# Down-projection: when its weight sums are formed in HBM, and where its Strassen products are combined

## The chip, the cores and the metric

One core of one Trainium2 chip runs the whole program. The metric is device time in microseconds of that core for one launch, lower is better. TensorE (PE in the profile) multiplies; VectorE (DVE), ScalarE (ACT) and GpSimd (POOL) do the elementwise work; SyncE (SP), ACT and POOL issue DMAs. PSUM is the memory of eight banks into which TensorE accumulates, SBUF the working memory, HBM the outer one.

## The reference

One layer of a hybrid token mixer and a convolutional feed-forward block (FFN) on 512 latent tokens of width 1024, with 256 context tokens as a prefix. Cut to its frame:

```python
sh1x, sc1x, g1x, sh2x, sc2x, g2x = split((silu(c) @ w_ada + b_ada), 6)
hx  = modulate(rms_norm(x, norm1_g), sh1x, sc1x)
x   = x + g1x * token_mixer(hx, ..., s_f, s_b)   # (sigmoid(ga)*(a@w_br_a) + sigmoid(gb)*(ob@w_br_b)) @ w_o
hx2 = modulate(rms_norm(x, norm2_g), sh2x, sc2x)
a, val = split(hx2 @ w_up, (D_FF, D_FF))         # D_FF = 2816
a   = depthwise_conv_3x3(a) + conv_b             # on an 8 x 64 grid
x   = x + g2x * ((gelu(a) * val) @ w_down)       # w_down: 2816 x 1024
return rms_norm(x, final_norm_g)
```

All inputs and the output are float32. The change touches when some sums of blocks of `w_down` are formed, the product with `w_down`, and the last lines.

## The kernel before

**Products in three passes.** Each float32 weight block arrives in SBUF as `raw` (128 x 1024), is rounded by ACT to `wh` (L223) and DVE forms the remainder `wl = raw - wh` (L224). Activations are split in the same way into a high and a low part. A product is then three matmuls (high x high, high x low, low x high), so one weight costs 24 matmuls of 128x512.

**The weight stream.** `specs` lists 155 weight blocks in the order of use: heads (0 to 9), VS and U (10 to 25), GA with `w_br_a` (26 to 41), R (42 to 49), GB with `w_br_b` (50 to 65, the last gate stage), `w_o` (66 to 73), `ffn_w_up` (74 to 117) and `w_down` (118 to 154). `weights()` (L241) hands out the next one; each call also splits up to two blocks ahead and loads up to four ahead (`raw` has 4 slots, `wh` and `wl` 5 each). The loads are issued by SP, in order.

**The modulation.** The vectors `g1`, `sh2`, `sc2`, `g2` are not needed until late, so `ada2` (L1157) runs in the background of the middle stages: a POOL memset of four accumulators (L1164), their bias by SP (L1166), 64 loads of `w_ada` pieces by SP (L1172, `wa`), DVE additions (L1173), and for each accumulator a split (L349, L350) and two matmuls (L1180, L1181). In SP's queue `wa` loads and weight loads alternate, and in DVE's queue the additions and the `wl` splits.

**The Strassen stage.** `w_down` is split in five blocks of 512 rows (`BLOCKS`), each a 2 x 2 of quarters (256 rows by 512 columns), and a rest of two 128-row tiles (`TAIL`). The output is likewise 2 x 2: tokens 0 to 255 or 256 to 511 by columns 0 to 511 or 512 to 1023. In Winograd's form the blocks take seven products in place of eight; each product is a pair of PSUM banks (one per 128 tokens) into which 60 matmuls go. Four of the products multiply by sums of quarters, which are made in HBM: `sums_build()` has 40 steps of 512 KB, each a DMA that POOL issues, 20 that copy a quarter and 20 that add (L192, L194; ten of these read another sum). `weights()` takes one step per call from the third call on. On the other side `all_preps()` forms the sums of activations and splits them. After each product DVE combines it with the earlier ones in SBUF: `taken` is an ACT copy of a bank, `combine` (L1557) a DVE addition or subtraction of a bank and a tile; `out_add` (L1501, L1502) multiplies by the gate `g2` and adds to the residual `x1`. Banks are taken in turn from two pools, `mm` and `gl`, of four each.

**The tail.** For each tile of 128 tokens `out_tok` ends the row: the sum of squares on ACT (L1507), `n3b` on DVE (L1518), the root on ACT (L1519), its reciprocal on DVE (L1520), then the left half times it on ACT (L1522, L1523 the DMA), the right half on DVE (L1524, L1525 the DMA). The last matmuls belong to tiles 2, 3, 0, 1 in this order.

What sets the order on an engine is the order in which the program is written out, moved by a scheduler; `in_order` pins some of it.

## Time and profile before

| | |
|---|---|
| median of 3 runs | 930.86 us (930.39 to 930.86) |
| profiled execution: its own time | 931.05 us |
| its span | 929.3 us |
| TensorE busy, of the span | 98% |
| DVE, ACT, POOL busy | 74%, 43%, 5% |
| granted TensorE clock | 0.999 |
| HBM read, written | 137.88 MB, 23.07 MB |

Times in the profile count from the span's start; the execution's own time holds the span and what lies around it. A row of the chain of waits is one piece of the work that ended last, with its start and length. Matmuls are pipelined: the 0.39 us of one is its way through, and the distance from start to start is what it costs. Times of landing are from a DMA's issue. "SPq", "POOLq" and "ACTq" are the queues of engines that issue DMAs.

### The profile page before, as it was taken

To read this page: it belongs to the slowest core of one execution; us is meant where nothing else is said; L and a number is where in the kernel's file an instruction comes from. 1 tells how busy PE (TensorE), PEld (TensorE's weight loads), DVE (VectorE), ACT (ScalarE), POOL (GpSimd) and SP (SyncE) were. 2 spreads that over 40 slices of the span, in tenths; PEclk is the share of its full clock that TensorE was granted. 3 is DMA by queue.
4 is the path that set the end of the run, shared out by engine and by line. 5 is a ranking of instruction groups with operands and counts; after the bars stand their busy time and mean duration, and the time that the engine had idled before them with its cause. 6 is when DMAs were issued, how large, how long until landed. Compare 5 with 4: busy or idle time off the path is not lost.

```text
span 929.3 us, 12172 instructions
## 1 busy us (share of the span) xinstructions
PE 913.0 (98%) x4540; PEld 761.3 (82%) x4540; DVE 690.7 (74%) x1197; ACT 400.8 (43%) x669; POOL 42.3 (5%) x74
## 2 busy tenths in 40 slices
PE   7999999999999999999999999999999999999996
PEld 5778888888888887788888888888888888888885
DVE  5578687779798644379665445898787878999796
ACT  5357465556542223223223226643343334465734
POOL 1200100010011112100000000000000000000000
PEclk9999999999999999999999999999999999999999
DMA  9951710662359999995452350533333333356642
GB/s 281 333 150 26 246 48 1 205 202 92 91 182 238 262 233 222 249 289 182 136 173 87 101 187 10 155 110 91 107 98 91 91 102 103 102 171 202 187 131 90
DMA packets 158615, 140.76 MB, mean 151 GB/s; under 512 B 6825, under 2 KB 122869, under 8 KB 158557
## 3 DMA queue, kind: packets, MB, share of 16 engines
q1 hardware_dynamic: 149197, 117.72, 41.4%
q0 software_dynamic: 8672, 21.19, 10.0%
q10 hardware_dynamic: 688, 1.09, 0.3%
q8 instruction: 35, 0.57, 0.2%
q14 instruction: 23, 0.19, 0.1%
HBM read 137.88 MB, written 23.07 MB: 173 GB/s over the span
## 4 chain that ended last, share of the span: by engine, by line
PE 85%; DMA 6%; DVE 4%; SPq 3%; ACT 1%; issue 1%; DVEq 0%; ACTq 0%
PE mm L357 48%; PE mm L375 11%; PE gl L1535 6%; PE mm L1535 4%; DMA wa<-in_w_ada_dram 3%; PE gl L881 3%; DMA raw<-in_w_in_dram 2%; SPq L273 1%; PE mm L988 1%; PE mm L1038 1%; PE mm L651 1%; PE gl L375 1%; DVE wl L224 1%; DVE vsn L1134 1%; SPq L294 1%; PE gl L916 1%
## 5 line engine op out<-in xcount | busy, mean ns | idle before, releaser
L223 ACT CAST wh<-raw 128x1024 fp32r<-128x1024 f32 x154 | 161.7, 1054 | 316.0 <-PE mm L357 180.9
L224 DVE TENSOR_TENSOR wl<-raw,wh 128x1024 fp32r<-128x1024 f32 x154 | 186.8, 1219 | 73.7 <-ACT wh L223 73.1
L357 PE MATMUL mm<-h2l,wh 128*128 128x512 f32 (+1 forms) x344 | 133.1, 387 | 0.0
L357 PE MATMUL mm<-h2h,wh 128*128 128x512 f32 (+1 forms) x344 | 133.1, 387 | 0.0
L357 PE MATMUL mm<-h2h,wl 128*128 128x512 f32 (+1 forms) x344 | 133.1, 387 | 0.0
L1392 DVE SCALAR_TENSOR_TENSOR cacc<-ca,ccol,cacc 128x441 f32<-128x441 f32 (+2 forms) x176 | 121.8, 694 | 4.1
L357 PE MATMUL mm<-hxh,wh 128*128 128x512 f32 x296 | 116.2, 392 | 0.0
L357 PE MATMUL mm<-hxh,wl 128*128 128x512 f32 x296 | 115.5, 390 | 0.0
L357 PE MATMUL mm<-hxl,wh 128*128 128x512 f32 x296 | 115.5, 390 | 0.0
L357 PEld LDWEIGHTS mm<-h2h,wl 128*128 128x128 f32 x344 | 64.6, 188 | 13.2
L357 PEld LDWEIGHTS mm<-h2h,wh 128*128 128x128 f32 x344 | 64.6, 188 | 13.1
L357 PEld LDWEIGHTS mm<-h2l,wh 128*128 128x128 f32 x344 | 64.6, 188 | 13.0
L1173 DVE SCALAR_TENSOR_TENSOR acc<-wa,cs,acc 128x512 f32<-128x512 f32 x64 | 46.0, 744 | 34.7 <-DMA wa<-in_w_ada_dram 34.6
L357 PEld LDWEIGHTS mm<-hxh,wl 128*128 128x128 f32 x296 | 55.6, 188 | 11.6
L357 PEld LDWEIGHTS mm<-hxh,wh 128*128 128x128 f32 x296 | 55.6, 188 | 11.1
L357 PEld LDWEIGHTS mm<-hxl,wh 128*128 128x128 f32 x296 | 55.6, 188 | 11.1
L1393 ACT ACTIVATE cacc<-cacc 128x512 f32<-128x512 f32 x22 | 13.9, 632 | 50.3 <-DVE cacc L1392 50.3
L375 PE MATMUL mm<-wh,hxh 128*128 128x512 f32 x88 | 34.7, 395 | 0.0
L375 PE MATMUL mm<-wl,hxh 128*128 128x512 f32 x88 | 34.4, 391 | 0.0
L375 PE MATMUL mm<-wh,hxl 128*128 128x512 f32 x88 | 34.3, 390 | 0.0
L1535 PE MATMUL gl<-wl,dah 128*128 128x512 f32 x80 | 31.1, 389 | 0.0
L1535 PE MATMUL gl<-wh,dah 128*128 128x512 f32 x80 | 31.1, 389 | 0.0
(429 smaller groups left out, 1729.9 us busy)
## 6 DMA issues: line engine op xcount, KB each, us to landing
raw<-in_w_in_dram SPq DMA_DIRECT2D x52, 512.0 KB, 4.3
wa<-in_w_ada_dram SPq DMA_DIRECT2D x96, 256.0 KB, 5.3
raw<-in_ffn_w_up_dram SPq DMA_DIRECT2D x44, 512.0 KB, 3.7
sum<-in_ffn_w_down_dram POOLq DMA_DIRECT2D x30, 512.0 KB, 6.1
raw<-sum SPq DMA_DIRECT2D x20, 512.0 KB, 3.8
raw<-in_ffn_w_down_dram SPq DMA_DIRECT2D x17, 512.0 KB, 3.6
sum<-sum POOLq DMA_DIRECT2D x10, 512.0 KB, 8.4
raw<-in_w_br_a_dram SPq DMA_DIRECT2D x8, 512.0 KB, 7.1
```

The lines of the kernel that those rows point to most:

```text
L223: A.copy(wh, raw)
L224: V.tensor_tensor(wl, raw, wh.bitcast(F32), op=ALU.subtract)
L273: dma(t_, w_ada[0, kp * nk * P:(kp + 1) * nk * P, c0:c0 + cg].rearrange("(k p) c -> p k c", p=P))
L294: dma(fqk[k // 2][0][:, j, k % 2], wi[k * P:(k + 1) * P, c0:c0 + P])
L357: T.matmul(ps, a[:, k, :], b[:, c0:c0 + n], start=(k == 0 and i == 0), stop=(k == KT - 1 and i == 2))
L375: T.matmul(ps, a[:, t * P:(t + 1) * P], b[:, k % 2, :], start=(k == 0 and i == 0), stop=(k == KT - 1 and i == 2))
L651: T.matmul(fps[i], a, b, start=(k == 0 and z == 0), stop=(k == KT - 1 and z == 2))
L881: T.matmul(ps, p_, q_, start=(start and z == 0), stop=(stop and z == 2))
L1173: V.scalar_tensor_tensor(acc[j], w_, cs[:, k, 0:1], acc[j], op0=ALU.mult, op1=ALU.add)
L1392: V.scalar_tensor_tensor(o, a_[:, r0 + dy:r1 + dy, c0 + dx:c1 + dx], wcol(tap), o, op0=ALU.mult, op1=ALU.add)
L1393: A.activation(acc, acc, AF.Gelu)
L1535: T.matmul(ps, a, w[:, kk, c0:c0 + n_], start=(first and kk == 0 and i == 0), stop=(last and kk == 1 and i == 2))
```

## The change

1. The 40 steps of `sums_build()` begin at weight 60 (`SUMS0`) and not at weight 2, one per call, so they go with weights 60 to 73 and 76 to 101 (74 and 75 are taken without a call).
2. The Strassen products keep their PSUM banks: X and Z are the `gl` pairs, Y is an `mm` pair. The first product M1 goes into X and is copied; M5 into Z and is copied; M6 is accumulated onto M1 in X, copied (`u2`) and subtracted from the right half of tokens 0 to 255; the third goes into Y with the first rest; X and Z go on accumulating likewise, with one copy or one `combine` between. `specs` and `all_preps()` follow the new order, and the last two quarters in row 1, column 1 come after the second sums.
3. The first rest's weights are held until both token halves have used them.
4. `out_tok` returns its last four operations as `finish`; tile 0's are run within tile 1's.

```diff
@@ -32,6 +32,7 @@
 TAIL = FT - 4 * BLOCKS
 LEAD = 5
 EARLY = 8
+SUMS0 = 60
 
 
@@ -171,14 +172,22 @@
     def w_block(ap):
         specs.append((ap.rearrange("(k p) c -> p k c", p=P), 2, 512))
 
-    by_block = lambda f: [w_block(f(b)) for b in range(BLOCKS)]
-    by_block(lambda b: quarter(b, 0, 0))
-    for i in range(4):
-        by_block(lambda b: sums[b][i])
-    for col in range(2):
-        by_block(lambda b: quarter(b, 1, col))
+    by_block = lambda f, b0=0, b1=BLOCKS: [w_block(f(b)) for b in range(b0, b1)]
+
+    def w_rest(col):
         for k in range(2 * BLOCKS, FT // 2):
             w_cols(ffn_w_down[0], col * 512, 512, 2 * k, 2)
+
+    by_block(lambda b: quarter(b, 0, 0))
+    by_block(lambda b: sums[b][0])
+    by_block(lambda b: sums[b][1])
+    by_block(lambda b: quarter(b, 1, 0))
+    w_rest(0)
+    by_block(lambda b: sums[b][3])
+    by_block(lambda b: quarter(b, 1, 1), 0, BLOCKS - 2)
+    by_block(lambda b: sums[b][2])
+    by_block(lambda b: quarter(b, 1, 1), BLOCKS - 2)
+    w_rest(1)
 
     def sums_build():
         for step in (((0, (0, 1)), (1, (1, 1)), (2, (1, 0)), (3, (0, 1))), ((0, (0, 0)), (3, (1, 1))),
@@ -241,7 +250,7 @@
     def weights():
         i = pos[2]
         pos[2] += 1
-        if i > 1:
+        if i >= SUMS0:
             next(building, None)
         stream_split(i + 2)
         stream_load(i + 1 + AHEAD)
@@ -1451,15 +1460,21 @@
         for b in range(BLOCKS):
             yield act_both(kept[b])
         for b in range(BLOCKS):
-            yield act_both(quads(b)[3])
+            yield act_both(quads(b)[1])
         for b in range(BLOCKS):
             a11, _, a21, _ = quads(b)
             yield act_both(tile_op(a11, a21, ALU.subtract))
+
+        def last(b):
+            V.tensor_tensor(kept[b], quads(b)[1], kept[b], op=ALU.add)
+            return act_both(kept[b])
+
+        for b in range(BLOCKS - 2):
+            yield last(b)
         for b in range(BLOCKS):
-            yield act_both(quads(b)[1])
-        for b in range(BLOCKS):
-            V.tensor_tensor(kept[b], quads(b)[1], kept[b], op=ALU.add)
-            yield act_both(kept[b])
+            yield act_both(quads(b)[3])
+        for b in range(BLOCKS - 2, BLOCKS):
+            yield last(b)
 
     preps, ready = all_preps(), []
 
@@ -1493,13 +1508,13 @@
         wh, wl = w
         for i, (a, b) in enumerate(((gh, wh), (gh, wl), (gl_, wh))):
             T.matmul(ps, a[:, t * P:(t + 1) * P], b[:, kk, c0:c0 + n], start=(first and i == 0),
-                     stop=(last and i == 2))
-
-    def out_add(pv, hf, t, c0, n):
+                     stop=(last and i == 2), skip_group_check=True)
+
+    def out_add(pv, hf, t, c0, n, op=ALU.add):
         tmp = late([P, n], s="yt")
         xv = x1[t][hf][:, c0:c0 + n]
         V.tensor_tensor(tmp, pv, bc_g["g2", hf][:, c0:c0 + n], op=ALU.mult)
-        V.tensor_tensor(xv, xv, tmp, op=ALU.add)
+        V.tensor_tensor(xv, xv, tmp, op=op)
         return tmp, xv
 
     def out_step(pv, hf, t, c0, n, part):
@@ -1519,10 +1534,14 @@
         A.activation(r, ss3[:, t, before:before + 1], AF.Sqrt, bias=b_, scale=1.0 / D)
         V.reciprocal(r, r)
         in_order(start, V.engine)
-        A.mul(xg[t], xg[t], r)
-        adma(out[0, t * P:(t + 1) * P, 0:512], xg[t])
-        V.scalar_tensor_tensor(x1[t][1], x1[t][1], r, fng[1], op0=ALU.mult, op1=ALU.mult)
-        dma(out[0, t * P:(t + 1) * P, 512:1024], x1[t][1])
+
+        def finish():
+            A.mul(xg[t], xg[t], r)
+            adma(out[0, t * P:(t + 1) * P, 0:512], xg[t])
+            V.scalar_tensor_tensor(x1[t][1], x1[t][1], r, fng[1], op0=ALU.mult, op1=ALU.mult)
+            dma(out[0, t * P:(t + 1) * P, 512:1024], x1[t][1])
+
+        return finish
 
     n, todo = [0], []
 
@@ -1533,7 +1552,7 @@
             hi, lo = (y.rearrange("p k t -> p (k t)")[:, c:c + P] for y in (ah, al))
             for i, (a, w) in enumerate(((hi, wh), (hi, wl), (lo, wh))):
                 T.matmul(ps, a, w[:, kk, c0:c0 + n_], start=(first and kk == 0 and i == 0),
-                         stop=(last and kk == 1 and i == 2))
+                         stop=(last and kk == 1 and i == 2), skip_group_check=True)
 
     def operands():
         prep(n[0] + LEAD)
@@ -1542,15 +1561,13 @@
         n[0] += 1
         return z
 
-    def products(bank, blocks=BLOCKS, stop=True):
-        banks = [bank() for _ in range(2)]
+    def products(banks, first=True, stop=False, blocks=BLOCKS):
         for b in range(blocks):
             z = operands()
             for t in range(2):
-                product_in(banks[t], t, 0, 512, z, b == 0, stop and b == blocks - 1)
+                product_in(banks[t], t, 0, 512, z, first and b == 0, stop and b == blocks - 1)
             if todo:
                 todo.pop(0)()
-        return banks
 
     def combine(a, b, op):
         t_ = late([P, 512], s="dc")
@@ -1562,51 +1579,64 @@
         A.copy(t_, ps)
         return t_
 
-    m1 = [taken(z) for z in products(gl)]
-    m5 = products(gl)
-    m6 = products(mm)
-    u2 = [combine(m, z, ALU.add) for z, m in zip(m6, m1)]
-    w5 = [combine(z, u, ALU.subtract) for z, u in zip(m5, u2)]
-    m4 = products(mm)
-    u4 = [combine(u, z, ALU.add) for u, z in zip(u2, m4)]
-    m7 = products(gl)
-    c21 = [combine(u, z, ALU.add) for u, z in zip(u4, m7)]
-    e22 = [combine(w, z, ALU.subtract) for w, z in zip(w5, m7)]
-    for t in range(4):
-        todo.append(lambda t=t: out_add((w5 + e22)[t], 1, t, 0, 512))
-    def rest_in(ps, t, c0, n_, w, first):
+    def rest_in(ps, t, w, first):
         for k in range(TAIL):
-            down(ps, gs[k], w[k // 2], k % 2, t, c0, n_, first and k == 0, k == TAIL - 1)
-
-    acc = products(gl, stop=False)
+            down(ps, gs[k], w[k // 2], k % 2, t, 0, 512, first and k == 0, k == TAIL - 1)
+
+    def left(t, src):
+        out_step(src, 0, t, 0, 512, 0)
+        xg.append(late([P, 512], s="xg"))
+        V.tensor_tensor(xg[t], x1[t][0], fng[0], op=ALU.mult)
+
+    X, Z = [gl() for _ in range(2)], [gl() for _ in range(2)]
+    Y = [mm() for _ in range(2)]
+    products(X)
+    m1 = [taken(z) for z in X]
+    products(Z, stop=True)
+    m5 = [taken(z) for z in Z]
+    products(X, False)
+    u2 = [taken(z) for z in X]
+    for t in range(2):
+        todo.append(lambda t=t: out_add(u2[t], 1, t, 0, 512, ALU.subtract))
+    products(Y)
     w = [weights() for _ in range(TAIL // 2)]
     start = len(traced())
     for g_ in gact:
         gs.append(split_act(g_.rearrange("p r w -> p (r w)"), s="g", lo_pool=late, eng=A.copy))
     A.activation(small(1, "root"), eps_t, AF.Sqrt)
     in_order(start, A.engine)
-    for t in range(4):
-        ps = acc[t] if t < 2 else mm()
-        rest_in(ps, t, 0, 512, w, t > 1)
-        e = (m1 + c21)[t]
-        V.tensor_tensor(e, ps, e, op=ALU.add)
-        out_step(e, 0, t, 0, 512, 0)
-        xg.append(late([P, 512], s="xg"))
-        V.tensor_tensor(xg[t], x1[t][0], fng[0], op=ALU.mult)
-
+    for t in range(2):
+        rest_in(Y[t], t, w, False)
+        left(t, combine(Y[t], m1[t], ALU.add))
+    products(X, False)
+    e22 = [combine(m, z, ALU.subtract) for m, z in zip(m5, X)]
+    for t in range(2):
+        todo.append(lambda t=t: out_add(e22[t], 1, t + 2, 0, 512))
     first = BLOCKS - 2
-    acc = products(mm, first, False)
+    products(Z, False, blocks=first)
+    products(X, False)
+    for t in range(2):
+        rest_in(X[t], t + 2, w, False)
+        left(t + 2, X[t])
     zs = [operands() for _ in range(BLOCKS - first)]
     w = [weights() for _ in range(TAIL // 2)]
     for t in (2, 3):
-        ps = gl()
-        rest_in(ps, t, 0, 512, w, True)
-        out_tok(t, lambda: out_step(ps, 1, t, 0, 512, 1), 1)
+        ps = mm()
+        rest_in(ps, t, w, True)
+        out_tok(t, lambda: out_step(ps, 1, t, 0, 512, 1), 1)()
+    ends = []
     for t in range(2):
         for z in zs:
-            product_in(acc[t], t, 0, 512, z, False, False)
-        rest_in(acc[t], t, 0, 512, w, False)
-        out_tok(t, lambda: out_step(acc[t], 1, t, 0, 512, 1), 1)
+            product_in(Z[t], t, 0, 512, z, False, False)
+        rest_in(Z[t], t, w, False)
+
+        def part():
+            out_step(Z[t], 1, t, 0, 512, 1)
+            while ends:
+                ends.pop()()
+
+        ends.append(out_tok(t, part, 1))
+    ends.pop()()
 
 
 # ---- launch: one core; inputs and outputs as the reference has them ----
```

**Where instructions move.** Three places, before and after apart. POOL, at the modulation's accumulators (`acc`) and the sums in HBM (`sum`); before:

```order
L192 DMA sum_128<-in_ffn_w_down_dram 256x512
L192 DMA sum_131<-in_ffn_w_down_dram 256x512
L1164 MEMSET acc_2952 128x512
L1164 MEMSET acc_2955 128x512
L1164 MEMSET acc_2958 128x512
L1164 MEMSET acc_2961 128x512
L192 DMA sum_132<-in_ffn_w_down_dram 256x512
```

after the change:

```order
L1173 MEMSET acc_2935 128x512
L1173 MEMSET acc_2938 128x512
L1173 MEMSET acc_2941 128x512
L1173 MEMSET acc_2944 128x512
L1173 MEMSET acc_3979 128x512
L1173 MEMSET acc_3982 128x512
L1173 MEMSET acc_3985 128x512
L1173 MEMSET acc_3988 128x512
L201 DMA sum_115<-in_ffn_w_down_dram 256x512
L201 DMA sum_116<-in_ffn_w_down_dram 256x512
```

The first memsets stood behind 17 sums and the second four behind 39; now all eight stand ahead of the first sum.

TensorE, at the change from the second Strassen product to the third (matmul 3888; `dah`, `dal` are the split sums of activations); before:

```order
L1535 MATMUL gl_7440<-wl_7515,dah_7443 128x512
L1535 MATMUL gl_7440<-wh_7514,dal_7444 128x512
L1535 MATMUL mm_7554<-wh_7536,dah_7466 128x512
L1535 MATMUL mm_7554<-wl_7537,dah_7466 128x512
L1535 MATMUL mm_7554<-wh_7536,dal_7467 128x512
```

after the change:

```order
L1554 MATMUL gl_7339<-wl_7517,dah_7445 128x512
L1554 MATMUL gl_7339<-wh_7516,dal_7446 128x512
L1554 MATMUL gl_7336<-wh_7538,dah_7468 128x512
L1554 MATMUL gl_7336<-wl_7539,dah_7468 128x512
L1554 MATMUL gl_7336<-wh_7538,dal_7469 128x512
```

The matmuls are the same; the third product went into a new bank (`mm_7554`) and now goes into the first product's (`gl_7336`), which an ACT copy has read.

DVE, the last rows of the program (x_1049 is the right half of token tile 0, x_1051 that of tile 1); before:

```order
L1501 TENSOR_TENSOR yt_8247<-mm_8118,g_1025_4928 128x512
L1502 TENSOR_TENSOR x_1049_5075<-x_1049_5075,yt_8247 128x512
L1518 TENSOR_SCALAR n3b_8245<-ss_7335 128x1
L1520 RECIPROCAL n3r_8246<-n3r_8246 128x1
L1524 TENSOR_SCALAR x_1049_5075<-x_1049_5075,n3r_8246,fng_7333 128x512
L1501 TENSOR_TENSOR yt_8278<-mm_8119,g_1025_4928 128x512
L1502 TENSOR_TENSOR x_1051_5079<-x_1051_5079,yt_8278 128x512
L1518 TENSOR_SCALAR n3b_8276<-ss_7335 128x1
L1520 RECIPROCAL n3r_8277<-n3r_8277 128x1
L1524 TENSOR_SCALAR x_1051_5079<-x_1051_5079,n3r_8277,fng_7333 128x512
```

after the change:

```order
L1516 TENSOR_TENSOR yt_8229<-gl_7338,g_1025_4890 128x512
L1541 TENSOR_SCALAR x_1055_5053<-x_1055_5053,n3r_8197,fng_7333 128x512
L1517 TENSOR_TENSOR x_1049_5041<-x_1049_5041,yt_8229 128x512
L1533 TENSOR_SCALAR n3b_8227<-ss_7335 128x1
L1535 RECIPROCAL n3r_8228<-n3r_8228 128x1
L1516 TENSOR_TENSOR yt_8256<-gl_7339,g_1025_4890 128x512
L1517 TENSOR_TENSOR x_1051_5045<-x_1051_5045,yt_8256 128x512
L1541 TENSOR_SCALAR x_1049_5041<-x_1049_5041,n3r_8228,fng_7333 128x512
L1533 TENSOR_SCALAR n3b_8254<-ss_7335 128x1
L1535 RECIPROCAL n3r_8255<-n3r_8255 128x1
L1541 TENSOR_SCALAR x_1051_5045<-x_1051_5045,n3r_8255,fng_7333 128x512
```

Tile 0's last product (L1524, now L1541) moved behind tile 1's addition, and tile 3's (x_1055) into tile 0's part.

## The prediction

> **What bounds the kernel now.** I read the page first, then the chain of waits from its end backwards, then TensorE's waits, and only then the rows around them.
>
> ```profile
> PE 913.0 (98%) x4540; PEld 761.3 (82%) x4540; DVE 690.7 (74%) x1197; ACT 400.8 (43%) x669; POOL 42.3 (5%) x74
> ```
>
> TensorE is busy for 98% of the span of 929.3 us, so anything that saves work on DVE, ACT or a queue is worth only what it takes out of TensorE's gaps. The chain of waits (start, length, what; longest pieces) says where these are:
>
> ```profile
> 334.34 8.75 DMA wa<-in_w_ada_dram
> ...
> 348.11 8.79 DMA wa<-in_w_ada_dram
> 357.00 0.76 DVE acc L1173
> ...
> 362.81 16.31 DMA raw<-in_w_in_dram
> ...
> 385.01 97.99 PE mm L357 x432
> ...
> 587.44 228.51 PE mm L357 x1008
> ...
> 922.06 0.70 DVE yt L1501
> ...
> 924.80 0.75 DVE x L1524
> ```
>
> From 385.01 us to the last matmul the chain is TensorE alone: 432 matmuls in 97.99 us, 0.2268 us each, 5.44 us for the 24 matmuls of one weight. Nothing that the change does to DVE there can bring a gain. Before 385 the chain goes through loads: the modulation loads `wa` (8.75 and 8.79 us) and one weight load of 16.31 us, with DVE sums of the modulation between. TensorE's own waits (total, times, longest) show what of that it felt:
>
> ```profile
> PE gl L1181 <- DVE accl L350: 1.4, 2, 1.1
> PE gl L1180 <- ACT acch L349: 0.6, 2, 0.3
> PE gl L1096 <- DVE swl L350: 0.3, 1, 0.3
> ```
>
> The first two are the modulation product of `ada2`; their idle times are counted from modelled ends of pipelined matmuls, so I measure the loss from start to start in TensorE's timeline (start, length, line):
>
> ```profile
> 357.81 0.39 PE L357 MATMUL mm<-ah,wl 128*128 128x512 f32 x1
> ...
> 359.18 0.50 PE L1181 MATMUL gl<-accl,ones_r 128*128 128x512 f32 x1 [0.23 <-DVE accl L350]
> 359.52 0.39 PE L357 MATMUL mm<-hxh,wh 128*128 128x512 f32 x1
> ```
>
> ```profile
> 382.14 0.39 PE L357 MATMUL mm<-ah,wl 128*128 128x512 f32 x1
> ...
> 384.51 0.51 PE L1181 MATMUL gl<-accl,ones_r 128*128 128x512 f32 x1 [1.14 <-DVE accl L350]
> 384.85 0.40 PE L357 MATMUL mm<-hxh,wh 128*128 128x512 f32 x1
> ```
>
> Each piece holds three matmul steps, worth 3 x 0.2268 = 0.68 us. The first takes 359.52 - 357.81 = 1.71 us (1.03 lost), the second 384.85 - 382.14 = 2.71 (2.03 lost): 3.06 us in all.
>
> **The change part by part. The sums leave 98 to 400 us.** Who makes the loads late is seen in the DMA queues of the stretch 318:357 (packets, MB, share of 16 engines; then issues, KB, median us to landing):
>
> ```profile
> q0 software_dynamic: 1683, 3.22, 51.1%
> ...
> wa<-in_w_ada_dram SPq DMA_DIRECT2D x12, 256.0 KB, 8.8
> ```
>
> and in 404:440, where POOL's queue is nearly empty:
>
> ```profile
> wa<-in_w_ada_dram SPq DMA_DIRECT2D x11, 256.0 KB, 5.1
> ```
>
> The software queue, which carries the sums, takes half of all DMA time there. The loads form a ring: a batch of four `wa` is issued, lands, DVE adds it, splits the next weight, and this frees the slots for the next batch. Its period was 348.11 - 334.34 = 13.77 and 362.81 - 348.11 = 14.70 us, while TensorE eats two weights in 2 x 5.44 = 10.89. With landings of 5.1 in place of 8.75 and 8.79 the periods are about 10.1 and 11.0, so the ring keeps up. The two rounds alone bring the modulation's `acc` some 7.3 us forward, and the first loss was 1.03; at the second the load of 16.31 us shrinks as well. Bounds of this term: 0 (the ring has another limit) and -3.52 (the wait of L1096 at 261 us goes too, 0.46 from start to start; but its chain is DVE's own work, so I leave it). I take **-3.06**, the value at the end nearest the rows, since less than a sixth of the expected lead would suffice at the first place.
>
> The Trainium skill ("DMA: Bandwidth & Descriptors", section "Queues, rings and completion order") says that each DMA engine takes turns between the queues that have work, a packet batch at a time. By it a load beside a sum takes up to twice its time alone, so `wa` would land in 4.4 us and the periods be 9.5 and 10.3; the measured ratio is 8.8 to 5.1, 1.7, and the sum would be the same.
>
> **The sums arrive at about 490 to 730 us.** Forty steps, one per weight of 5.44 us: six in the last gate stage, eight in `w_o`, 26 in the FFN. What one costs is the software queue's time over the span divided by 40: 10.0% of 929.3 / 40 = 2.3 us of all 16 engines, thus 2.3 / 5.44 = 0.43 of the DMA's time more.
>
> ```profile
> q0 software_dynamic: 8672, 21.19, 10.0%
> ...
> raw<-in_ffn_w_up_dram SPq DMA_DIRECT2D x44, 512.0 KB, 3.7
> ```
>
> ```profile
> 600.00:640.00 40.00, 40.00 (x178) 33.14 (x177) 36.07 (x54) 17.29 (x24) 0.00 (x0) 1.00 0.32 94
> ```
>
> The row of the windows (us; busy PE, PEld, DVE, ACT, POOL; clock; DMA share; GB/s) gives 0.32 there, so 0.75 with the sums. What hides it is the lead of the weight loads (SP's and ACT's timelines):
>
> ```profile
> 644.75 33.01 SPq L211 DMA_DIRECT2D raw<-in_ffn_w_up_dram  x7
> ```
>
> ```profile
> 663.44 1.06 ACT L223 CAST wh<-raw 128x1024 fp32r<-128x1024 f32 x1 [3.23 <-PE mm L357]
> ```
>
> The first of these seven loads is the one that the cast at 663.44 reads (`raw` has four slots, and the three casts between belong to the loads before): 18.7 us after its issue, 15.0 after its landing, and what releases the cast is TensorE, not the load. If a sum brings the landing to 8.8, 10 us of cover are left. The cast itself runs four weights (21.8 us) ahead of its use. A landing of over 18 us would be needed before even a cast is late: cost **0**. The finished sums are first read at about weight 120 (after 815 us); the last is issued near weight 99.
>
> **The modulation's memsets** now stand ahead of all sums in POOL's queue; nothing waits behind a sum there any more. A gain at most, and the same 3.06.
>
> **The Strassen stage** has the same 468 matmuls of 128x512, and ten DVE additions fewer against four ACT copies more. TensorE is dense there, so the ten (about 0.68 us each) are worth 0. Can the new order stop it? A bank goes on accumulating only after its copy: X is read after its first product and written again 60 matmuls (13.6 us) later, the shortest gap is the 36 matmuls (8.2 us) into Z between two uses of X, and a copy or an addition takes 0.6 to 0.7 us:
>
> ```profile
> L1562 ACT COPY dt<-gl 128x512 f32<-128x512 f32 x2 | 1.2, 584 | 0.1
> L224 DVE TENSOR_TENSOR wl<-raw,wh 128x1024 fp32r<-128x1024 f32 x32 | 38.9, 1219 | 7.2 <-ACT wh L223 6.7
> L1557 DVE TENSOR_TENSOR dc<-dc,gl 128x512 f32<-128x512 f32 x4 | 2.5, 678 | 0.0
> ```
>
> The weight pair of the first rest is held from matmul 4008 to 4187, so four of five pairs turn over. From a freed pair to its next need are then 36 matmuls, 8.2 us, against 0.42 (matmul start to reader, 922.06 - 921.64) + 1.06 (cast) + 1.22 (`wl`) = 2.7: 5.5 us to spare. The tightest place is where DVE waits for the last matmul into X (4079) to form `e22`, with six operations and a `wl` behind it that TensorE needs at 4117: 38 x 0.2268 = 8.6 us against 0.42 + 6 x 0.68 + 1.22 = 5.7, so 2.9 to spare. Cost **0**, bounds 0 and what the third rival gives.
>
> **The tail.** Token tile 0's last multiplications and output DMAs are moved behind tile 1's addition. DVE's 0.75 (L1524) then lies between tile 1's `x` and its `n3b`, while ACT squares:
>
> ```profile
> 921.64 0.39 PE L1495 MATMUL mm<-wh,gl 128*128 128x512 f32 x1
> ...
> 923.40 0.15 DVE L1518 TENSOR_SCALAR n3b<-ss 128x1 f32<-128x1 f32 x1
> 923.51 0.63 ACT L1507 ACTIVATE yt<-x 128x512 f32<-128x512 f32 x1 [2.07 <-DVE x L1502]
> 924.27 0.29 ACT L1519 ACTIVATE n3r<-ss,n3b 128x1 f32<-128x1 f32 x1
> ...
> 924.80 0.72 ACT L1522 ACTIVATE xg<-xg,n3r 128x512 f32<-128x512 f32 x1 [0.23 <-DVE n3r L1520]
> ...
> 925.55 0.37 ACTq L1523 DMA_DIRECT2D out_dram<-xg  x1
> ```
>
> `n3b` ends near 924.2 instead of 923.55, and is needed at 924.27: just hidden. But ahead of it tiles 2 and 3 now share their additions, which by my reckoning with these durations pushes tile 0's reciprocal to about 922.05, the moment at which tile 1's `yt` may start; that costs about 0.2. Tile 0's output DMAs are then issued some 1.4 us before the last ones, instead of four, and may share DMA time with them: 0 to 0.3. Bounds 0 and 1.84 (0.75 of DVE, 0.72 of ACT's multiplication and 0.37 of its issue all in series); I take **+0.3**.
>
> **Sum**: 931.05 (the profiled execution's own time) - 3.06 + 0 + 0 + 0.3 = 928.3. The median of the runs, 930.86, lies 0.19 below that execution, so **928.1 us** on it, 0.30% less. About 0.2%, 1.86 us, is what a measurement of this kernel can tell from no change: under 929.0 is faster, over 932.7 slower.
>
> **The rivals.** 1. *The ring stays bound by something else.* For it: the page's row of DMA shares (40 slices of 23.2 us, in tenths) is full from the thirteenth slice to the eighteenth, 279 to 418 us, and SP's own loads, let go earlier, could fill what the sums leave:
>
> ```profile
> DMA  9951710662359999995452350533333333356642
> ```
>
> Against: the software queue's 51.1%, and 5.1 us landings with as many loads but no sums. If only the second loss goes, 931.05 - 2.03 + 0.3 - 0.19 = 929.1; if neither, 931.2. It decides if two rounds gain under 1 us together.
>
> 2. *The tail takes the bound of 1.84*: 930.86 - 3.06 + 1.84 = 929.6. For it: reciprocal and `yt` meet within 0.1 us in my reckoning. Against: most of the moved work has ACT and DVE idle to run in.
>
> 3. *Slower: DVE is behind in the Strassen stage.* Its place is the `wl` behind `e22` (and the same after the first rest). For it: DVE is nearly full at its entry,
>
> ```profile
> 820.00:860.00 40.00, 40.00 (x179) 33.10 (x178) 38.24 (x50) 25.33 (x34) 0.00 (x0) 1.00 0.67 201
> ```
>
> with 1.76 us idle of 40. Each microsecond of backlog over 2.9 stops TensorE for one. Slower by the bound needs a stall of 3.06 - 0.3 + 1.86 = 4.6, a backlog of 7.5. At 10 us the stall is 7.1 and the time 928.1 + 7.1 = 935.2. Against: the change takes 10 x 0.68 = 6.8 us off DVE in this very stage.
>
> 4. *Slower: each sum that POOL issues in the FFN holds DVE.* DVE has 3.9 us idle of 40, thus 13.8 in the 141 us of 26 weights, and 21.8 - 2.3 = 19.5 us of lead; so it takes 33.3 / 26 = 1.28 us for each sum before TensorE waits. At two issue lengths (1.76 each, 45.8 in all) the end is 12.5 us late: 940.6. Against, in the timelines of POOL and DVE:
>
> ```profile
> 333.05 0.88 POOL L194 DMA_DIRECT2D sum<-in_ffn_w_down_dram  x1 [1.05 <-DVE acc L1173]
> ```
>
> ```profile
> 332.66 2.35 DVE L224 TENSOR_TENSOR wl<-raw,wh 128x1024 fp32r<-128x1024 f32 x2
> ```
>
> two `wl` with the issue of a sum in their midst take 1.18 each, no more than the mean of 1.22. The Trainium skill ("SBUF — State Buffer", section "SBUF: two separate sides") speaks for this rival: DVE and GpSimd share a port pair that one of them holds for a whole instruction while the other waits. These two rows show no such wait.
>
> **How the numbers follow.** Forecast 0.67 (927.4 to 929.0: the 0.46 at 261 going too, or the tail at its worse half), rival 1 0.13, rival 2 0.09, rival 3 0.06, rival 4 0.05. Faster 0.67; within the bound 0.13 + 0.09 = 0.22; slower 0.06 + 0.05 = 0.11. The range of 8 in 10 starts below the forecast's and takes in the first two rivals: **927.2 to 931.2**.
>
> **What would show it.** Right: no rows of L1181 and L1180 in TensorE's waits (or 0.1), `wa` landing in 4 to 6 us between 318 and 357, TensorE's chain unbroken from about 262 us on; DMA share about 0.75 at 600:640 with casts still released by TensorE; 24 matmuls in 5.44 us through the Strassen stage; from the last matmul to the span's end 7.7 to 8.3 us (929.3 - 921.64 = 7.66 now). Wrong: a TensorE wait on `accl` that stays with the sums gone (rival 1), a last piece over 9 us (2), a wait on `wl` or on an X bank after 816 us (3), or `wl` rows of over 1.3 us beside POOL's issues (4).

## The result and the profile after

The changed kernel takes 926.39 us, median of four runs (926.02 to 928.11), against 930.86 of the kernel before (four runs, 930.39 to 931.88): the ratio is 0.9954, with a 95% interval of 0.9937 to 0.9971. It is faster, as forecast, but by 4.5 us and not 2.8, and lies below the range that began at 927.2. A later measurement of the same kernel gave a ratio of 0.9963 (0.9950 to 0.9976); its medians were 925.95 and, for the kernel before, 930.45.

The profiled execution took 928.11 us for a span of 925.1, against 931.05 and 929.3 before. Its page and TensorE's waits (total, times, longest):

```profile
PE 910.6 (98%) x4540; PEld 760.5 (82%) x4540; DVE 683.8 (74%) x1187; ACT 403.6 (44%) x673; POOL 42.5 (5%) x74
```

```profile
PE mm L421 <- DMA rows<-in_b_ada_dram: 6.5, 1, 6.5
PE gl L660 <- ACT hxh L599: 0.3, 1, 0.3
PE mm L660 <- ACT wh L539: 0.2, 1, 0.2
```

After the start nothing waits any more: the modulation's two waits are gone, and so is the one on `swl` (0.3 by this view, 0.46 from start to start) which the prediction left standing. The three that are left lie before 79 us and are in both kernels. The chain of waits of the two kernels can be laid side by side at landmarks, first the kernel before:

```profile
79.50 5.67 PE mm L1038 x24
...
276.63 5.46 PE mm L357 x24
...
385.01 97.99 PE mm L357 x432
...
587.44 228.51 PE mm L357 x1008
...
920.67 1.37 PE mm L1495 x6
```

and the changed one:

```profile
78.96 5.67 PE mm L1047 x24
...
275.31 5.46 PE mm L366 x24
...
380.73 97.97 PE mm L366 x432
...
583.14 228.51 PE mm L366 x1008
...
916.37 1.37 PE gl L1510 x6
```

The lead of the changed kernel grows 0.54, 1.32, 4.28, 4.30, 4.30 us. So there are three pieces: 0.54 before 79 us, where both programs are the same; 0.78 between 79 and 276; and 2.96 between 276 and 385. From the FFN on, through the Strassen stage to the last matmuls, nothing. Since the first 79 us vary from execution to execution (below), the experiments are compared by the distance D from the 24 matmuls at 79 us to the FFN's 1008: 587.44 - 79.50 = **507.94** before, 583.14 - 78.96 = **504.18** after, 3.76 less.

The ring of the modulation's loads now keeps TensorE's pace. SP's timeline of the changed kernel:

```profile
316.41 2.00 SPq L1181 DMA_DIRECT2D wa<-in_w_ada_dram  x4
...
327.29 1.99 SPq L1181 DMA_DIRECT2D wa<-in_w_ada_dram  x4
...
338.16 2.21 SPq L1181 DMA_DIRECT2D wa<-in_w_ada_dram  x4
```

A batch every 10.88 us, exactly two weights at 5.44: the loads wait for TensorE and not the other way round. In the DMA view of 318:357 `wa` lands in 4.5 us where it took 8.8:

```profile
wa<-in_w_ada_dram SPq DMA_DIRECT2D x9, 256.0 KB, 4.5
```

The idle time of DVE ahead of the additions of `wa` that the page puts down to these loads falls from 34.6 to 3.2 us. (In the names of tiles, `swl`, `accl`, `obh` and so on, an `h` or `l` at the end marks the high or the low part of a split; `vsn`, `o`, `var` and `gp` are tiles of the stages in between.) What the prediction overlooked stands in the timelines of POOL and DVE, of the kernel before

```profile
258.37 0.56 POOL L192 DMA_DIRECT2D sum<-in_ffn_w_down_dram  x1 [32.55 <-DVE vsn L1134]
258.92 1.96 POOL L1164 MEMSET acc<- 128x512 f32 x4
```

```profile
259.19 1.83 DVE L1143 TENSOR_SCALAR o<-o,var 128x256 f32<-128x256 f32 x1
260.94 0.67 DVE L350 TENSOR_TENSOR swl<-swT,swh 128x512 fp32r<-128x512 f32 x1
```

and of the changed one:

```profile
245.06 1.92 POOL L1173 MEMSET acc<- 128x512 f32 x4 [194.98 <-ACT junk L977]
```

```profile
258.64 0.33 DVE L1152 TENSOR_SCALAR o<-o,var 128x256 f32<-128x256 f32 x1
258.90 0.67 DVE L359 TENSOR_TENSOR swl<-swT,swh 128x512 fp32r<-128x512 f32 x1
```

The same operation took 1.83 us before and 0.33 now. Before, it ran into POOL's memsets of the accumulators and ended 0.14 us after them (261.02 against 260.88); `swl`, for which TensorE waited, came behind it, and so did a second `swl`. That is why more is lost than the 0.46 at the first: from the matmul ahead of the first `swl` product to the group behind the second, TensorE takes 2.15 us before (260.99 to 263.14) and 1.39 after (260.43 to 261.82), 0.76 less. The memsets ran there because they stood in POOL's queue behind a sum that waited for DVE's `vsn`; now no sum is ahead of them and they run 14 us earlier. The sums themselves are where they were expected, at a higher DMA share than the 0.75 worked out (changed kernel; us, busy of PE, PEld, DVE, ACT, POOL, clock, DMA share, GB/s):

```profile
600.00:640.00 40.00, 40.00 (x178) 33.13 (x177) 36.42 (x54) 15.30 (x21) 5.68 (x8) 1.00 0.81 197
640.00:680.00 40.00, 40.00 (x178) 33.12 (x177) 31.39 (x46) 15.14 (x20) 7.11 (x8) 1.00 0.92 196
```

### The profile page after: what moved, and what is told of

Same layout as the page of the kernel before. It is cut to its first block, busy times and chain, and to the rows that moved or that the text cites. A ratio compares the mean times of both kernels' runs of the same rounds, so it can differ in the third digit from the quotient of the medians.

```text
span 925.1 us, 12162 instructions
## 1 busy us (share of the span) xinstructions
PE 910.6 (98%) x4540; PEld 760.5 (82%) x4540; DVE 683.8 (74%) x1187; ACT 403.6 (44%) x673; POOL 42.5 (5%) x74
## 4 chain that ended last, share of the span: by engine, by line
PE 97%; DMA 1%; ACT 0%; SPq 0%; DVE 0%; issue 0%; ACTq 0%
PE mm L366 56%; PE mm L384 12%; PE gl L1554 9%; PE gl L890 3%; PE mm L660 2%; PE mm L1554 1%; PE gl L660 1%; PE mm L997 1%; PE mm L1047 1%; PE gl L384 1%; PE gl L569 1%; PE gl L925 1%; PE gl L1213 1%; DMA wa<-in_w_ada_dram 1%; PE gl L366 1%; PE mm L377 1%
## 5 line engine op out<-in xcount | busy, mean ns | idle before, releaser
L1554 PE MATMUL gl<-wh,dah 128*128 128x512 f32 x120 | 46.7, 389 | 0.0
L1554 PE MATMUL gl<-wl,dah 128*128 128x512 f32 x120 | 46.7, 389 | 0.0
L1554 PE MATMUL gl<-wh,dal 128*128 128x512 f32 x120 | 46.7, 389 | 0.0
```

The lines of the kernel that those rows point to most:

```text
L1554: T.matmul(ps, a, w[:, kk, c0:c0 + n_], start=(first and kk == 0 and i == 0), stop=(last and kk == 1 and i == 2), skip_group_check=True)
```

## The experiments

Ratios are to the kernel before on the same chip, with 95% intervals.

**1. Only the sums late.** In the kernel before:

```diff
-        if i > 1:
+        if i >= 60:
             next(building, None)
```

> The kernel before with one line changed: the sums in HBM begin at weight 60; products, banks and tail stay as before. Theory A (all of the gain comes from when the sums are issued): 926.4 us, within 0.5 of the changed kernel, no TensorE waits on accl, acch or swl, and the FFN's 1008 matmuls begin 4.3 us earlier than the 587.44 of before, give or take 0.6. Theory B (the new combination of the Strassen products or the new tail bring a part of it): 927.5 us or more, with the FFN still beginning 4.3 us earlier.

926.35 us, 0.9952 (0.9939 to 0.9966), D = 504.18, no waits on `accl`, `acch`, `swl`. Theory A: one number makes the whole gain.

**2. Only the new products and the new tail.** In the changed kernel:

```diff
-SUMS0 = 60
+SUMS0 = 2
```

> The changed kernel with the sums beginning at weight 2 again; the new products, banks and tail stay. Theory A: 930.5 to 931.3 us, as before: TensorE waits on accl and acch for about 3 us between 340 and 400 us and on swl near 261. Theory B: 929.5 us or less, with the Strassen stage or the tail shorter than in the kernel before (from the start of its first matmul, 815.95, to the span's end: 113.4 us).

930.8 us, 1.0002 (0.9992 to 1.0011), D = 508.15. The waits are those of the kernel before:

```profile
PE gl L1190 <- DVE accl L359: 1.5, 2, 1.3
PE gl L1189 <- ACT acch L358: 0.7, 2, 0.5
...
PE gl L1105 <- DVE swl L359: 0.3, 1, 0.3
```

From the first Strassen matmul to the end nothing is gained: ten DVE operations less are worth nothing beside a dense TensorE.

**3. The memsets held where they were.** In the changed kernel, `vsn_last` being the last `vsn` instruction:

```diff
-                G.memset(a_, 0.0)
+                start = len(traced())
+                for _ in range(1):
+                    G.memset(a_, 0.0)
+                for i in traced()[start:]:
+                    if i.engine == G.engine and part == 0:
+                        tc.add_manual_dep(i, vsn_last.name, mybir.DependencyInfo(
...
```

> The changed kernel, with POOL's first four memsets of the modulation's accumulators held until the last vsn of DVE, where they stood before (there behind a sum). Sums stay late. Theory P (while POOL's memset runs, DVE's SBUF-to-SBUF operations wait whole): the first scaling of o by DVE behind the two swT copies takes over 0.9 us instead of 0.33 and ends with the last memset, swl is as much later, TensorE waits there, and 0.3 to 0.8 us are lost up to 270 us: 926.7 to 927.2. Theory Q (POOL's queue and DVE do not meet; DVE's burst ended earlier for another reason): o 0.33, no wait, 926.4.

925.92 us, 0.9948 (0.9935 to 0.9960), D = 504.22. POOL, then DVE:

```profile
256.30 1.92 POOL L1176 MEMSET acc<- 128x512 f32 x4 [207.58 <-DVE vsn L1143]
```

```profile
256.04 1.31 DVE L1096 COPY swT<-gl 128x512 f32<-128x512 f32 x2
257.24 1.13 DVE L1153 TENSOR_SCALAR o<-o,var 128x256 f32<-128x256 f32 x1
258.29 0.67 DVE L359 TENSOR_TENSOR swl<-swT,swh 128x512 fp32r<-128x512 f32 x1
```

The first `o` is held to the memset's end (258.22, `o` 258.37), as theory P says, but here 0.80 us, and TensorE had that much to spare; in the kernel before the sum's issue put the memsets later and the hold was 1.50. The mechanism is there; the loss that the theory expected is not. The copies of `swT`, which read PSUM, ran beside the memsets in 1.31 us, and in 1.27 without them in the changed kernel.

**5. The same, the dose doubled.** Each held memset is issued twice (`range(2)`).

> The changed kernel with the held memsets of the third experiment each issued twice, eight in a row behind the last vsn (about 3.9 us). There the four took 1.92 us, the scaling of o 1.13 instead of 0.33, and TensorE did not wait. Theory P: the first o now takes 2.8 to 3.3 us and ends with the last memset; swl is 2.5 to 3 us later than without, TensorE waits on swl, and the distance from the 24 matmuls at 79 us to the FFN's 1008 grows from the changed kernel's 504.2 by 1.5 to 2.3 us. Theory Q (o was long by chance): 504.2 again, o 0.3 to 1.2.

928.11 us, 0.9972 (0.9961 to 0.9983), D = 506.28.

```profile
257.20 3.79 POOL L1176 MEMSET acc<- 128x512 f32 x8 [207.60 <-DVE vsn L1143]
```

```profile
258.15 2.99 DVE L1153 TENSOR_SCALAR o<-o,var 128x256 f32<-128x256 f32 x1
```

```profile
PE gl L1105 <- DVE swl L359: 1.4, 1, 1.4
```

`o` took 2.99 us, again to the end of the memsets, and D grew by 2.1. With holds of 0, 0.80, 1.50 and 2.66 us the losses are 0, 0, 0.8 and 2.1: about one for one above 0.7. The stretch from the 24 matmuls at 79 us to those at 276 has this piece alone. It is 197.13 us in the kernel before and 197.14 and 197.15 in experiments 2 and 7, whose memsets run as late; 198.45 with the dose doubled; and 196.32 to 196.40 in every other trace but that of experiment 8, which loses its time in this stretch. Experiments 6 and 12, which keep the sums early, and experiment 3 with its hold of 0.80 are among them. That settles the second piece of the gain, 0.7 to 0.8 us.

**4. The sums beside the modulation, the memsets ahead of them.** In the changed kernel:

```diff
-SUMS0 = 60
+SUMS0 = 26
```

> The changed kernel with the sums beginning at weight 26, the first gate stage, beside the modulation's loads, while the first memsets stay ahead of them. Theory A (the sums' DMAs beside the wa loads make the ring slower than TensorE): wa landing of 8 us or more, TensorE waits on accl of at least 2 us in all between 330 and 420 us, but none at 261 us: 928.5 to 931 us. Rival (what counts is only that the sums do not stand ahead of the memsets in POOL's queue): 926.4 us.

937.37 us, 1.0060 (1.0042 to 1.0078), D = 515.37: slower than both kernels, and by more than the theory allowed. No loss at 261 us, but not at 357 to 385 either, where the theory put it: beside the first ring only sums that copy run, and at a DMA share of 0.91 `wa` lands in 6.1 us. The loss is in the modulation's second ring, beside sums that add:

```profile
PE gl L1190 <- DVE accl L359: 3.6, 1, 3.6
PE mm L366 <- DVE obh L358: 1.9, 1, 1.9
```

```profile
440.00:460.00 20.00, 17.85 (x72) 14.09 (x71) 15.85 (x22) 5.68 (x7) 0.23 (x1) 0.91 0.80 228
...
480.00:500.00 20.00, 16.36 (x61) 12.88 (x60) 9.93 (x16) 3.11 (x4) 3.55 (x4) 0.83 0.88 208
```

DVE stands 6.11 us for a `wa` at 426.57 and 5.13 at 485.04, and works without a pause from the first of these until `obh` is late. The granted clock falls to 0.91 and 0.83 behind the waits, so each wait costs once more: TensorE's timeline after the longer one shows eleven matmuls at 0.427 us from start to start, not 0.227, until 492.39, which is 2.2 us. Not all of this is the sums' DMA: only the first four memsets are ahead of the sums here. The second four stood behind them in POOL's queue and ran at 383.88 (before 346 in the changed kernel), and the second ring's loads began at 386.12 us and not at 384.51.

```profile
483.07 0.40 PE L1189 MATMUL gl<-acch,ones_r 128*128 128x512 f32 x1
487.11 0.79 PE L1190 MATMUL gl<-accl,ones_r 128*128 128x512 f32 x1 [3.64 <-DVE accl L359]
487.70 0.63 PE L366 MATMUL mm<-hxh,wh 128*128 128x512 f32 x1
```

**6 and 12. The kernel before with the memsets ahead.** One call takes no step, so that the memsets pass the sum that waits for `vsn`:

```diff
-        if i > 1:
+        if i > 1 and i != 18:
             next(building, None)
```

> The kernel before, with one call (weight 18) that takes no step of the sums, so the first four memsets of the modulation stand ahead of the sum that waits for DVE's vsn; all sums still run beside the modulation's loads. Theory P: the first o 0.33 us, no TensorE wait on swl, and the distance from the 24 matmuls at 79 us to the FFN's 1008 falls from 507.9 by 0.7 to 507.2; the waits on accl and acch (3.06 us from start to start) stay. Otherwise: 507.9.

> The sixth experiment's kernel again (before, with the first memsets ahead of the sum that waits for vsn), for a second trace: the first was of the fastest of its ten runs and lost only 0.87 us at accl, where the kernel before lost 3.06 with a ring that began 12 us later. Theory R (the earlier start gives the ring a lead that the slower loads then use up): the loss at accl and acch is again 0.5 to 1.3 us, distance from the 24 matmuls at 79 us to the FFN's 1008 near 505. Theory S (the small loss was one execution's luck): 2 us or more, distance 506.5 to 507.5, as the median of 929.55 against 930.45 suggests.

929.55 us, 0.9993 (0.9979 to 1.0007), and 927.5 us, 0.9966 (0.9951 to 0.9980); D = 505.07 and 506.52. In both the wait on `swl` is gone, as theory P says; but D fell below the expected 507.2, since less was lost at the modulation. There the two executions differ, first the one execution, then the other:

```profile
PE gl L1181 <- DVE accl L350: 0.6, 1, 0.6
```

```profile
PE gl L1181 <- DVE accl L350: 1.2, 1, 1.2
PE gl L1180 <- ACT acch L349: 0.5, 1, 0.5
```

The first of the two losses (1.03 us at 357) is absent in one and 0.2 in the other; the ring's loads begin some 11 us earlier here, counted from the 24 matmuls at 79 us, and this lead may be what was used up later. The second loss (2.03 before) was 0.9 and 2.2. The second trace fits theory S, 2.4 us lost in all and 506.52: the small loss of the first belongs to that execution, the fastest of ten that took 926.57 to 932.21 us, while the second trace is of the slowest of five (926.79 to 929.45). The ring's loss thus varies from execution to execution, and how much of it an early start saves stays open.

**7. The sums paused while the ring runs.**

```diff
-        if i > 1:
+        if i > 1 and not 24 <= i < 60:
             next(building, None)
```

> The kernel before, with the sums paused from weight 24 to weight 59, that is while the modulation's loads run; the first memsets still stand behind the sum that waits for vsn. Theory A: waits on accl and acch gone, the wait on swl stays: distance from the 24 matmuls at 79 us to the FFN's 1008 of 507.9 - 3.06 = 504.9. If the sums before weight 24 matter too: more than 505.5.

927.61 us, 0.9969 (0.9957 to 0.9982), D = 504.97, the one of the three waits that is left being

```profile
PE gl L1096 <- DVE swl L350: 0.3, 1, 0.3
```

This is the ring's piece alone: 507.94 - 504.97 = 2.97, with 0.79 left for the memsets. The memsets were as late as before (258.71), so a late ring is no harm by itself.

**8. All sums early.** In the kernel before, three steps per call:

```diff
             next(building, None)
+            next(building, None)
+            next(building, None)
```

> The kernel before with three steps of the sums per weight from weight 2 on, so that all 40 are issued by weight 15 and done before the modulation's loads begin at 262 us. Theory A (the collision with the ring costs, not that the sums are early): the distance from the 24 matmuls at 79 us to the FFN's 1008 is that of the changed kernel, 504.2, within 0.2, unless the memsets fall into DVE's burst again (504.9); time 926 to 927.5 us. Rival (sums in the first 250 us cost something themselves, DMA share there then about 0.9): over 506, with new TensorE waits on weights before 250 us.

943.62 us, 1.0143 (1.0123 to 1.0164), D = 520.94. A miss for both: no new wait before 250 us, yet 14.5 us in one piece. POOL's timeline:

```profile
275.45 0.88 POOL L194 DMA_DIRECT2D sum<-sum  x1 [5.30 <-DMA sum<-sum]
276.01 2.25 POOL L1166 MEMSET acc<- 128x512 f32 x4
```

```profile
281.98 1.55 DVE L1175 SCALAR_TENSOR_TENSOR acc<-wa,cs,acc 128x512 f32<-128x512 f32 x2 [15.58 <-DMA wa<-in_w_ada_dram]
```

The sums wait on POOL for earlier ones to land, so 40 steps in a row are a chain, and the memsets at its end came 31 us later than in the changed kernel (276.01 against 245.06). SP's loads wait for them, DVE for the loads, and behind DVE's `acc` stands work that TensorE needs. Whether DMA contention before 250 us costs anything was thereby not tested against the ring, but TensorE did not wait there.

**9. The sums twice as fast in their new place.** In the changed kernel `next(building, None)` stands twice.

> The changed kernel with two steps of the sums per weight from weight 60 on, so that 12 steps fall into the last gate stage, 16 beside w_o and 12 into the first FFN weights, at twice the DMA rate. Theory A (weight loads have 10 us or more of cover in these stages): no new TensorE waits, distance from the 24 matmuls at 79 us to the FFN's 1008 of 504.2, within 0.2, 926 us. Rival (the cover is thin, the contention only sits where it is just hidden): TensorE waits on wh or wl between 480 and 640 us, 2 us or more lost.

926.83 us, 0.9966 (0.9955 to 0.9977), D = 504.00, as theory A says. Between 585 and 680 us weight loads land in 7.2 us (3.7 in the kernel before) at a DMA share of 0.90, and TensorE waits for no weight. One small wait is new, at 599.99 us, of DVE's `gp`; ACT's timeline shows what is behind it:

```profile
PE mm L367 <- DVE gp L1408: 0.4, 1, 0.4
```

```profile
592.81 1.05 ACT L232 CAST wh<-raw 128x1024 fp32r<-128x1024 f32 x1 [5.57 <-DMA raw<-in_ffn_w_up_dram]
```

Loads issued between 555 and 600 us land in 11.1 us. This cast waited 5.57 us for its load; DVE's `wl` waited for the cast, and in DVE's queue the work up to `gp` stands behind it. The distance from the 24 matmuls at 79 us to the last matmul grows by 0.6 us. So the cover that was worked out for the middle of the FFN is narrower at its entry: casts wait for loads there in the changed kernel too (1.35 us at 586.26, 1.69 at 589.00) and in the kernel before, beside no sums (1.42 us at 590.63, 1.41 at 593.10), without a loss for TensorE.

**10. The tail in place.** In the changed kernel:

```diff
-        ends.append(out_tok(t, part, 1))
-    ends.pop()()
+        out_tok(t, part, 1)()
```

> The changed kernel with token tile 0's last products and output DMAs back in their own part, not within tile 1's. The prediction gave the deferral a cost of 0.3 us; the changed kernel's trace shows 2.77 us from tile 1's yt to its last product against 2.74 before. Theory D (the deferral costs nothing, hidden under ACT's square): from the last matmul's start to the span's end 7.6 to 7.8 us, as with it (7.76). Theory E (it costs 0.3): 7.4 to 7.5.

926.74 us, 0.9967 (0.9956 to 0.9979), D = 504.16; from the last matmul's start (917.13) to the end 7.97 us. Neither theory: in place, the tail is 0.2 longer than deferred, since tile 0's product now stands in front of tile 1's `yt`:

```profile
917.14 0.75 DVE L1541 SCALAR_TENSOR_TENSOR x<-x,n3r,fng 128x512 f32<-128x512 f32 x1
917.81 0.68 DVE L1516 TENSOR_TENSOR yt<-gl,g 128x512 f32<-128x512 f32 x1
```

**11. The changed kernel again.**

> The changed kernel unchanged, in five rounds, for a second trace and a better ratio. If the change is worth the 3.76 us by which the distance from the 24 matmuls at 79 us to the FFN's 1008 shrank (507.94 to 504.18), and the rest of the difference of the medians is the spread of the first 79 us, that distance is 504.2 again, the 24 matmuls at 79 us begin anywhere from 77.6 to 79.5, and the ratio is near 0.9960.

925.95 us, 0.9963 (0.9950 to 0.9976), D = 504.15, and the 24 matmuls begin at 78.11. Over 14 traces, alike in the order up to there, they begin between 77.59 and 79.50, the latest being the profiled execution of the kernel before. So 504.2 repeats, and the ratio is, as expected, near 0.9960.

No version beat the changed kernel by more than this spread; the first experiment equals it.

## Why the prediction was wrong, and where it was right

**What bounds the kernel, and the ring (-3.06): right.** D falls by 2.97 when only the sums beside the ring go (7), and both waits vanish. The ring's period, estimated at 10.1 and 11.0, is 10.88, TensorE's pace. (By the rule that the prediction quotes, the first period would be 9.4 and not 9.5; nothing hangs on it.) Rival 1 did not come.

**The memsets: here it failed.** "A gain at most, and the same 3.06", and of the wait at 261 us: "its chain is DVE's own work, so I leave it". The chain was DVE's, but one link of it took five times its length, and why was to be seen in the neighbour's timeline: `o` 1.83 us where the others of its kind take 0.33, beside POOL's memsets. The failed step is thus the term for the memsets and the wait behind them: it was taken as 0, stood in the bound of -3.52 with 0.46, and measured -0.7 to -0.8, since both `swl` came late. The prediction knew of a port that DVE and POOL may share, weighed it against the sums alone, found no sign in two `wl`, and did not try it on the one POOL operation that the change moves past a DVE burst. `wl` is a two-input operation; `o` is of another kind.

**The tail (+0.3): too high.** From the last matmul to the span's end are 7.76 us, 7.66 before: +0.1. The rows of the changed kernel show the hold that was reckoned with, hidden under ACT as expected:

```profile
919.10 0.74 DVE L1541 SCALAR_TENSOR_TENSOR x<-x,n3r,fng 128x512 f32<-128x512 f32 x1
919.22 0.63 ACT L1522 ACTIVATE yt<-x 128x512 f32<-128x512 f32 x1 [1.15 <-DVE x L1517]
...
919.76 0.14 DVE L1533 TENSOR_SCALAR n3b<-ss 128x1 f32<-128x1 f32 x1
920.00 0.29 ACT L1534 ACTIVATE n3r<-ss,n3b 128x1 f32<-128x1 f32 x1
```

`yt` starts 0.42 us after the last matmul's start, as before; tile 0's reciprocal came 0.6 us ahead of it, not at the same moment. Deferring is worth 0.2 in the new order (10). Rival 2 did not come.

**The sums in their new place (0): right**, with the DMA share at 0.81 to 0.92 and not 0.75. That no cast would be late below a landing of 18 us holds for the loads it was read from, not for the FFN's entry: at twice the rate a landing of 11.1 us made a cast late and cost 0.6 us (9). Rival 4 did not come: DVE is hardly busier at 600:640 (36.42 us of 40 against 36.07), and the mean of a `wl` is 1.221 us against 1.219.

**The Strassen stage (0): right.** FFN to last matmul is the same in both kernels, and experiment 2 has it alone. Rival 3 did not come.

**The sum again**, with the measured terms: 931.05 - 3.0 - 0.75 + 0.1 - 0.19 = 927.2, the edge of the range. So the memsets alone do not explain a time below it; 0.8 us are left to 926.39, and where they come from stays open. Two things have the size. The 24 matmuls at 79 us begin 77.59 to 79.50 us into the span, and the trace that the sum starts from is the latest: 0.54 of the 4.30 us between the two traces arose before 79 us, where the change moves nothing. And the ring's loss varies: the stretch from the matmuls at 276 us to the FFN is longer than in the changed kernel by 3.0 us in the trace of the kernel before, 3.2 in experiment 2, 0.9 and 2.3 in 6 and 12. So other executions of the kernel before may lose more than the profiled one. The repetition leaves the same doubt: by its ratio the change is worth 3.4 us, by its medians 4.5. The range did reach past the bound of -3.52 with a free tail (927.3); it had no room for the second `swl` or for these two spreads.

## What to carry to other kernels

A background DMA is cheap or dear by the lead of the loads that it meets, and not by the free DMA time alone: at a share of 0.8 to 0.9 beside weight loads with some 15 us of cover these sums cost nothing, and at a share near 1 (318 to 357 us in the kernel before) beside a ring of loads that frees its own slots they cost 3 us. Even the ring bore the sums that copy, at a share of 0.91 (experiment 4). Look for the place with the least cover, here the FFN's entry and not its middle. In an in-order queue ask of every instruction behind a waiting one (here a memset behind a sum) where it now falls, and compare each operation with its siblings: one `o` of 1.83 us among others of 0.33 is a wait that no view of waits lists.

## What the runs showed of the hardware

A POOL memset holds a DVE operation that scales an SBUF tile into SBUF whole until it ends: 1.13, 1.83 and 2.99 us in place of 0.33, each ending 0.14 or 0.15 us after the memsets. A small copy of `var` between SBUF tiles was held as well: 0.34 or 0.35 us in the eight traces where it runs into the end of the memsets (246.66 to 247.01 in the changed kernel, whose memsets end at 246.98), 0.16 or 0.17 in the six others. DVE copies from PSUM (1.31 us for two beside the memsets, 1.27 without) were not held. The two-input `wl` that began just ahead of the memsets in the changed kernel (244.85) and ran beside them took 1.17 us, mean 1.22, and the four memsets took 1.92, as many as they took in experiment 3: neither held the other. The Trainium skill ("SBUF — State Buffer", section "Who interferes with whom") says just this: single-input DVE operations between SBUF tiles can run in a mode that takes the port pair shared with GpSimd, and whoever comes second waits for the other's whole instruction; operations with two inputs mind only a GpSimd operation that reads SBUF, and a memset does not. All rows above agree.

TensorE at half pace after waits: behind 4.04 us from start to start (experiment 4, at 483.07) eleven matmuls took 0.427 us each, behind the 2.31 us at 445.35, with a second short wait after them, six did; behind 1.84 us (experiment 5, at 259.95) and 1.70 us (experiment 12, at 381.25) none. The Trainium skill ("TensorE: Matmul & The Clock Gate", section "What's actually happening") states a half clock after an idle window of some 3.4 us; here 2.3 us and the short wait behind them were enough. These few cases do not show where the bound lies.
